# A decoder step on one core: the bias table's chain begun ahead of the first projection step, that step's products reordered, and the squares' gate moved

## The chip, the cores and the metric

The kernel runs on one core of a Trainium2 chip. The metric is the device time of one execution in microseconds; three runs of the kernel before took 2097.12, 2097.62 and 2098.48 us. The engines are called by their names or as the profile shortens them: TensorE (PE, its weight loads PEld), VectorE (DVE), ScalarE (ACT), GpSimd (POOL) and SyncE (SP). DMAs are issued by SP, ACT and POOL and run on 16 DMA engines.

## What is computed

One inference step of a one-layer decoder trunk on 2048 prompt positions with 16 meta tokens ahead of them, and on 8 sample rows. Cut to what matters here:

```python
h = rmsnorm(x, norm1_g)
p = h @ w_in                     # q 512 | k 128 | v 128 | conv a 512 | conv b 512
s = q.k / 8 + rel_bias[t5_bucket(distance)]    # window of 128, 8 heads, learned sinks
o = softmax(s, with sink) @ v
u = a * sigmoid(b)               # then a causal depthwise conv, 31 taps, LayerNorm, swish
x = x + concat(o, c) @ w_out
x = x + relu(rmsnorm(x) @ w_up)**2 @ w_down
y = rmsnorm(x)
```

The relative-position bias is the same table for every block of queries: for each head a row of 384 values by distance, which has to be laid out as a skewed matrix of 128 queries by 256 keys.

## The kernel before

**Tiles and products.** The positions are cut into five tiles (400, 448, 448, 448 and 328 columns); activations lie transposed, channels on partitions, in eight chunks `x[c]`. Weights come in slabs of 128 x 1024 numbers (512 KB): `raw` is loaded by SP, ScalarE casts it to a rounded high part `whi` (line 138), and VectorE subtracts to a low part `wlo` (line 115). Activations are split the same way into `hi` and `lo`. A projection step (`pe_step`) is 24 matmuls into one PSUM buffer: for eight chunks `whi`*`hi`, `whi`*`lo` and `wlo`*`hi`. There are two `raw` buffers, three pairs `whi`/`wlo`, and three PSUM buffers of the kind `mm` (steps 4 and 5 borrow two of another kind). The slabs are called 1, 2, 3 ... here in order of use; step k uses slab k, as long as tile 0 alone is worked on.

**The start.** `norm1_first` loads slab 1, the eight chunks of tile 0 and slab 2, and splits tile 0 times the gain, without its norm. The norm's scale `rs` is worked out beside the first steps: squares on ScalarE (`norm_stats`, held back by a one-element copy from a gate tile), their sum on VectorE (`ss`), column sums on TensorE (`st<-ones,ss`), a root and a reciprocal (`rq`), a diagonal (`m<-idn,rq`), a product that spreads it over the partitions (`st<-m,ones`), and a copy from PSUM by ScalarE (`t<-st`, 128x400). Each step's result of tile 0 waits in PSUM until VectorE has multiplied it by `rs` (`m<-mm,t`); the first such copy frees the PSUM buffer that step 6 needs. Meanwhile GpSimd issues the eight loads of tile 1 (`t<-x_in`), each behind a one-element copy from the last high part of tile 0.

**The bias chain.** `bias_setup` (line 937) multiplies the table by a one-hot matrix on TensorE (`st<-relt`), copies the 8 x 384 result from PSUM with ScalarE, and GpSimd issues its DMAs: `scr` (for the sample rows), `skw` (16 shifted copies in DRAM), one read for the sample rows, and eight reads of `skw` into `bias`, which wait for `skw` to have landed. It is called before the second step (`BAT = 1`). The first user of `bias` is the attention of tile 0 (`attn_gen`, line 576, a VectorE operation that adds it to the scores and takes the maximum).

**The order.** The program is written once, and a scheduler sets each engine's order from it at build time; a part under `high_priority` is drawn ahead. Each engine then works through its own order, and waits at an instruction until its operands are there.

Of the kernel before, what the change touches and what calls it, by code (L numbers as in the profile page):

```python
# [18 lines left out]
NH = 8  # L19
# [60 lines left out]
def trunk(tc, x_in, w_all, smalls, rel, ck, cv, sconv, y_out, kv_out, ck_out, cv_out, up_out, us_out):  # L80
    nc = tc.nc
    with ExitStack() as ctx:
# [10 lines left out]
        def ahead(gen, off, cond=None):  # L93
            while True:
                try:
                    if off and (cond is None or cond()):
                        with tc.high_priority(off):
                            r = next(gen)
                    else:
                        r = next(gen)  # L100
                except StopIteration:
                    return
                yield r
# [39 lines left out]
        def slot(dt=F32, i=None):  # L143
            t = tp.tile([128, TS], dt, tag="t", name="t")
            return t[:, SHIFT[i]:] if i in SHIFT else t
# [45 lines left out]
        def split_slab():  # L191
            k = pos["split"]
            if k >= len(order):
                return
            while pos["dma"] <= k:
                dma_slab()
            r = raws.pop(k)
            hi = sl.tile([128, 8, 128], F32R, tag="whi", name="whi", bufs=NSPL)
            lo = sl.tile([128, 8, 128], F32R, tag="wlo", name="wlo", bufs=NSPL)
            cpy(hi, r)  # L200
            tt(lo, r, f(hi), ALU.subtract)
            split[k] = (hi, lo)
            pos["split"] += 1
# [10 lines left out]
        def pe_step(hi, lo, n, evac, budget, late=False, parts=1, keep=False, spare=False):  # L214
            k = cur[0]
            if not keep:
                cur[0] += 1
            while pos["split"] <= min(k + LA, len(order) - 1):
                split_slab()
            while pos["dma"] < min(k + LA + 1 + NRAW, len(order)):  # L220
                dma_slab()
            if late:
                flush()
            wh, wl = split[k] if keep else split.pop(k)
            if spare:
                ps = pa.tile([128, 512], F32, tag="pt", name="mm")
            else:
                ps = pm.tile([128, 512], F32, tag="mm", name="mm")
            o = ps[:, :n]
            seq = []  # L230
            if late:
                for c in range(8):
                    seq += [(wh, hi, c), (wh, lo, c), (wl, hi, c)]
            else:
                for c in range(8):
                    seq += [(wh, hi, c), (wh, lo, c)]
                seq += [(wl, hi, c) for c in range(8)]
            cut = [len(seq) * (p + 1) // parts for p in range(parts)]
            for j, (w, a, c) in enumerate(seq):
                mm(o, w[:, c, :], a[c], j == 0, j == len(seq) - 1)  # L240
                if j + 1 == cut[0]:
                    old = list(pend)
                    pend.clear()
                    for e in old:
                        e()
                if j + 1 in cut:
                    bg.step(budget / parts)
            pend.append(lambda: evac(ps))
# [68 lines left out]
        def run_stats(gen, box):  # L317
            for r in gen:
                if r is None or r is STEP:
                    yield r  # L320
                else:
                    box.append(r)
# [42 lines left out]
        def norm1_first():  # L365
            s = st[0]
            n = TI[0]
            dma_slab()
            x = s["x"] = load_x(0)
            dma_slab()  # L370
            with tc.high_priority(2000):
                split_slab()
                warm = misc()
                for _ in range(WARM):
                    mm(warm[:, :128], ones, ones, True, True)
                s["h1h"], s["h1l"] = [], []
                for c in range(8):
                    hi = slot(F32R)
                    lo = slot(F32R)
                    act(hi[:, :n], x[c][:, :n], AF.Copy, scale=sm[:, G1 + c:G1 + c + 1])  # L380
                    stt(lo[:, :n], x[c][:, :n], sm[:, G1 + c:G1 + c + 1], f(hi[:, :n]), ALU.mult, ALU.subtract)
                    s["h1h"].append(hi)
                    s["h1l"].append(lo)
            split_slab()
            g1 = norm1_gen(1)
            next(g1)
            box = []
            s["rs"] = slot()
            for _ in ahead(run_stats(norm_stats(x, n, quick="a0" in QUICK, gate=s["h1h"][7], out=s["rs"]), box), 2000):
                pass  # L390
            return g1

# [541 lines left out]
                q.dma_start(y_out[:, YO[i] + c * n:YO[i] + (c + 1) * n], y[:, :n])  # L934
                yield

        def bias_setup():
            ps = misc()
            mm(ps[:NH, :EW], relt[:33, 0:NH], relt[:33, 8:8 + EW], True, True)
            e = slot()  # L940
            cpy(e[:NH, :EW], ps[:NH, :EW])
            nc.gpsimd.dma_start(scr.rearrange("p h x -> h p x"),
                                e[:NH, :EW].unsqueeze(1).broadcast_to([NH, NSMP, EW]))
            a = skw[:]
            row = NH * SKWW
            nc.gpsimd.dma_start(bass.AP(tensor=a.tensor, offset=a.offset, ap=[[SKWW, NH], [row + 1, NSKW], [1, EW]]),
                                e[:NH, :EW].unsqueeze(1).broadcast_to([NH, NSKW, EW]))
            for q in range(0, 128, NSKW):
                nc.gpsimd.dma_start(bias[q:q + NSKW], bass.AP(tensor=a.tensor, offset=a.offset + 127 - q,
                                                              ap=[[row, NSKW], [SKWW, NH], [1, 256]]))  # L950
# [80 lines left out]
        for op in prog:  # L1031
            k = op[0]
            if k == "in":
                _, i, m = op
                if i == 0:
                    if nin == N1AT:
                        gens["n1"] = [bg.add(g1)]
                    if nin == BAT:
                        bias_setup()
                    nin += 1  # L1040
                win_step(i, m, 24 * (TI[i] / 2400.0) - 1.2 - 0.6, spare=i == 0 and nin in (4, 5))
            elif k == "in2":
                m = op[1]
                win_step(0, m, 24 * (TI[0] / 2400.0) - 1.2 - 0.6, keep=True)
                win_step(1, m, 24 * (TI[1] / 2400.0) - 0.6)
            elif k == "conv0":
                flush()
                gens["conv"] = [bg.add(ahead(conv_gen(0), HP0, lambda: "ln" in st[0])), bg.add(conv_pe_gen(0), True)]
            elif k == "attn0":
                flush()  # L1050
                gens["attn"] = [bg.add(attn_gen(0, range(j, PT[0] // BQ[0], NS0)), A0F) for j in reversed(range(NS0))]
            elif k == "out":
                _, i, m = op
                wout_step(i, m, ff_budget(i, False))
            elif k == "ff":
                _, i, t, g, c = op
                b = ff_budget(i, t == "u")
                if t == "u":
                    up_step(i, g * 8 + c, b)
                else:  # L1060
                    down_step(i, g, c, b)
            elif k == "bg":
                i = op[1]
                flush()
                cat_alloc(i)
                gens["attn"] = [bg.add(attn_gen(i, range(j, PT[i] // BQ[i], NS1))) for j in range(NS1)]
                if i == NT - 1:
                    gens["attn"].append(bg.add(sample_gen(i)))
                gens["conv"] = [bg.add(ahead(conv_gen(i), HPC, lambda: "ln" in st[i]))]
            elif k == "sync_bg":  # L1070
                flush()
                bg.drain(gens["attn"] + gens["conv"])
            elif k == "n1":
                gens["n1"] = [bg.add(norm1_gen(op[1]))]
            elif k == "sync_n1":
                bg.drain(gens["n1"])
            elif k == "n2":
                gens["n2"] = [bg.add(ahead(norm2_gen(op[1]), HPN if op[1] else HPN0))]
            elif k == "sync_n2":
                flush()  # L1080
                bg.drain(gens["n2"])
            elif k == "fin":
                gens["fin"] = [bg.add(ahead(final_gen(op[1]), HPF if op[1] == NT - 1 else 0))]
                if op[1] == NT - 1:
                    flush()
                    bg.drain()
# [16 lines left out]
HPN0 = 300  # L1103
HPF = 0
COV = 5
BAT = 1
WARM = 12
N1AT = 3
A0F = True
# [118 lines left out]
```

## Time and profile before

| | |
|---|---|
| runs | 2097.12, 2097.62, 2098.48 us; median 2097.62 |
| profiled execution | 2097.54 us, of which the span is 2095.7 us |
| busy: PE, PEld | 2068.3 us (99%), 1961.5 us (94%) |
| busy: DVE, ACT, POOL | 1525.2 us (73%), 1181.0 us (56%), 55.8 us (3%) |
| chain that ended last | PE 95%, DVE 2%, DMA 1%, ACT 1% |
| granted clock of TensorE, mean | 0.993 |

The span is the time between the first and the last instruction that the profile shows; the execution's own time is 1.8 us longer. Busy times are sums over the whole span; the change touches the first 60 us of it. In the profile's rows a start is in us from the start of the span, and what stands in square brackets is the time for which the engine was idle before the row, and what ended that.

### The profile page before, as it was taken

How to read it: one execution, taken by the hardware profiler on the slowest of the kernel's cores; microseconds unless marked ns; L12 is line 12 of the kernel's file. 1: busy time of each engine (PE TensorE's matmuls, PEld its weight loads, DVE VectorE, ACT ScalarE, POOL GpSimd, SP SyncE). 2: the span in 40 equal slices, each digit the busy share in tenths (PEclk: the TensorE clock that was granted, in tenths of full speed). 3: DMA queues.
4: the chain of work that ended last, by engine and by line, in shares of the span. 5: the costliest groups of instructions: out<-in, count | busy, mean ns of one | idle time of the engine just before them, and what ended most of it. 6: DMA issues, size and time to landing. Idle time of an engine off the chain costs nothing.

```text
span 2095.7 us, 30054 instructions
## 1 busy us (share of the span) xinstructions
PE 2068.3 (99%) x11354; PEld 1961.5 (94%) x11354; DVE 1525.2 (73%) x2603; ACT 1181.0 (56%) x2154; POOL 55.8 (3%) x111
## 2 busy tenths in 40 slices
PE   9899999999999999999999999999999999999998
PEld 8688899999999999999999999999999999999997
DVE  7896798977858987658669886567797754564444
ACT  7577565667456456564454647555646465454443
POOL 3000000000000000000000000000011000000000
PEclk9899999999999999999999999999999999999999
DMA  7113233334532222234323222244433322444443
GB/s 209 47 37 111 100 122 104 128 114 160 179 111 101 101 101 101 101 136 162 129 104 108 101 101 101 101 172 150 142 117 112 123 105 101 151 162 151 151 143 105
DMA packets 77536, 254.39 MB, mean 121 GB/s; under 512 B 9661, under 2 KB 20037, under 8 KB 77392
## 3 DMA queue, kind: packets, MB, share of 16 engines
q1 hardware_dynamic: 72000, 238.08, 32.5%
q0 software_dynamic: 4672, 13.65, 2.3%
q8 instruction: 89, 1.46, 0.3%
q10 hardware_dynamic: 720, 0.76, 0.1%
q14 instruction: 55, 0.45, 0.1%
HBM read 241.97 MB, written 10.47 MB: 120 GB/s over the span
## 4 chain that ended last, share of the span: by engine, by line
PE 95%; DVE 2%; DMA 1%; ACT 1%; issue 0%; POOL 0%; SPq 0%; DVEq 0%; ACTq 0%; POOLq 0%
PE mm L159 89%; PE st L159 2%; PE pt L595 1%; PE s L159 1%; DVE t L119 1%; DMA bias<-skw 0%; DMA skw<-t 0%; DVE t L115 0%; PE cps L159 0%; DVE m L119 0%; ACT p L135 0%; DMA raw<-w_all 0%; DVE p L576 0%; DMA sm<-smalls 0%; ACT L134 0%
## 5 line engine op out<-in xcount | busy, mean ns | idle before, releaser
L159 PE MATMUL mm<-t,whi 128*128 128x448 f32 (+3 forms) x6560 | 1330.9, 349 | 3.1 <-ACT t L138 0.8
L159 PEld LDWEIGHTS mm<-t,whi 128*128 128x128 f32 x6560 | 1164.1, 188 | 58.2 <-DVE t L115 2.9
L138 ACT CAST whi<-raw 128x1024 fp32r<-128x1024 f32 x424 | 443.5, 1049 | 546.6 <-PE mm L159 430.2
L159 PE MATMUL mm<-t,wlo 128*128 128x448 f32 (+3 forms) x3280 | 702.6, 347 | 0.0
L115 DVE TENSOR_TENSOR wlo<-raw,whi 128x1024 fp32r<-128x1024 f32 x424 | 516.6, 1218 | 224.7 <-PE mm L159 123.5
L159 PEld LDWEIGHTS mm<-t,wlo 128*128 128x128 f32 x3280 | 587.9, 188 | 24.9
L119 DVE SCALAR_TENSOR_TENSOR t<-u,sm,t 128x448 f32<-128x448 f32 (+1 forms) x480 | 300.5, 645 | 3.5
L115 DVE TENSOR_TENSOR t<-mm,t 128x448 f32<-128x448 f32 (+2 forms) x200 | 116.5, 583 | 184.5 <-PE mm L159 181.4
L115 DVE TENSOR_TENSOR t<-m,t 128x448 fp32r<-128x448 f32 (+3 forms) x236 | 134.1, 581 | 25.8 <-ACT t L138 25.1
L138 ACT CAST t<-m 128x448 fp32r<-128x448 f32 (+3 forms) x236 | 125.3, 536 | 18.8 <-DVE m L119 14.6
L134 ACT ACTIVATE m<-mm 128x448 f32<-128x448 f32 (+2 forms) x176 | 90.2, 512 | 51.0 <-PE mm L159 49.5
L134 ACT ACTIVATE m<-t 128x448 f32<-128x448 f32 (+3 forms) x140 | 71.7, 542 | 61.7 <-DVE t L115 43.0
L134 ACT ACTIVATE m<-m 128x448 f32<-128x448 f32 (+3 forms) x164 | 90.1, 549 | 4.5 <-DVE m L115 0.6
L135 ACT ACTIVATE p<-p,nm 112x240 f32<-112x240 f32 (+3 forms) x152 | 72.3, 477 | 27.3 <-DVE nm L124 25.9
L576 DVE CUSTOM_DVE_ANT_0 p<-s,bias,sm 112x240 f32<-112x240 f32 (+3 forms) x152 | 61.1, 449 | 6.2 <-DMA bias<-skw 3.8
L134 ACT ACTIVATE p<-p,rd 112x240 f32<-112x240 f32 (+3 forms) x152 | 61.9, 476 | 3.9 <-DVE rd L130 3.5
L115 DVE TENSOR_TENSOR ss<-ss,m 128x448 f32<-128x448 f32 (+3 forms) x100 | 58.4, 584 | 6.3 <-ACT m L134 2.8
L934 POOL DMA_DIRECT2D y_out<-t x32 | 17.3, 543 | 1602.6 <-DVE t L119 1601.4
L130 DVE RECIPROCAL rs<-m 128x448 f32<-128x448 f32 (+2 forms) x15 | 41.6, 2776 | 23.9 <-ACT m L134 23.9
L119 DVE SCALAR_TENSOR_TENSOR t<-t,sm 128x384 f32<-128x384 f32 (+1 forms) x98 | 58.3, 612 | 0.9
L159 PE MATMUL mm<-cal,whi 128*128 128x448 f32 (+2 forms) x160 | 55.3, 347 | 0.2 <-DVE cal L115 0.2
L159 PE MATMUL mm<-cah,whi 128*128 128x448 f32 (+2 forms) x160 | 55.3, 347 | 0.0
(178 smaller groups left out, 1159.6 us busy)
## 6 DMA issues: line engine op xcount, KB each, us to landing
raw<-w_all SPq DMA_DIRECT2D x424, 512.0 KB, 3.2
t<-x_in SPq DMA_DIRECT2D x40, 224.0 KB, 4.6
y_out<-t POOLq DMA_DIRECT2D x24, 224.0 KB, 3.3
t<-x_in SPq DMA_DIRECT2D x16, 164.0 KB, 3.5
t<-x_in POOLq DMA_DIRECT2D x8, 224.0 KB, 4.3
t<-x_in SPq DMA_DIRECT2D x8, 200.0 KB, 4.6
t<-x_in SPq DMA_DIRECT2D x8, 192.0 KB, 3.8
y_out<-t POOLq DMA_DIRECT2D x8, 192.0 KB, 4.7
```

Source lines behind the costliest of these rows:

```text
L115: return nc.vector.tensor_tensor(out, a, b, op=op)
L119: return nc.vector.scalar_tensor_tensor(out, a, s, b, op0=op0, op1=op1)
L130: return nc.vector.reciprocal(out, a)
L134: return nc.scalar.activation(out, a, f, bias=bias, scale=scale)
L135: return nc.scalar.activation(out, a, f, bias=bias, scale=scale, accum_out=accum_out)
L138: return nc.scalar.copy(out, a)
L159: return nc.tensor.matmul(out, lhsT, rhs, start=start, stop=stop)
L576: nc.vector.tensor_tensor_reduce(out=p[:bq, c, :nk], in0=sp[c // 2][:bq, c % 2, :nk], in1=bias[:bq, h, b0:b0 + nk], scale=1.0, scalar=sm[: ...
L595: nc.tensor.transpose(t[:r, c * bq:(c + 1) * bq], p[:bq, c, a:a + r], idn[:bq, :bq])
L934: q.dma_start(y_out[:, YO[i] + c * n:YO[i] + (c + 1) * n], y[:, :n])
```

## The change

Three things. `bias_setup` is called in `norm1_first`, inside the part that is drawn ahead, right behind the split of tile 0, with the last high part as a gate: a one-element copy by GpSimd into the tile that takes the table's copy. Its product goes into a PSUM buffer of the kind that scores use. The first step's 24 products are written in another order: chunk by chunk as the operands come, and no longer all products of `whi` ahead of those of `wlo`. And the squares of tile 0 are gated by the last low part, where it was the last high part. What is computed stays the same.

```diff
@@ pe_step
             seq = []
-            if late:
+            if k == 0:
+                for c in range(9):
+                    if c < 8:
+                        seq += [(wh, hi, c)]
+                    if c > 0:
+                        seq += [(wl, hi, c - 1), (wh, lo, c - 1)]
+            elif late:
                 for c in range(8):
                     seq += [(wh, hi, c), (wh, lo, c), (wl, hi, c)]
@@ norm1_first
                     s["h1h"].append(hi)
                     s["h1l"].append(lo)
+                bias_setup(s["h1h"][7])
             split_slab()
...
-            for _ in ahead(run_stats(norm_stats(x, n, quick="a0" in QUICK, gate=s["h1h"][7], out=s["rs"]), box), 2000):
+            for _ in ahead(run_stats(norm_stats(x, n, quick="a0" in QUICK, gate=s["h1l"][7], out=s["rs"]), box), 2000):
                 pass
@@ bias_setup
-        def bias_setup():
-            ps = misc()
+        def bias_setup(gate):
+            ps = pa.tile([128, 512], F32, tag="s", name="bs")
             mm(ps[:NH, :EW], relt[:33, 0:NH], relt[:33, 8:8 + EW], True, True)
             e = slot()
+            nc.gpsimd.tensor_copy(e[:NH, :1], f(gate[:NH, :1]))
             cpy(e[:NH, :EW], ps[:NH, :EW])
@@ the program's loop
-                    if nin == BAT:
-                        bias_setup()
                     nin += 1
@@ constants
-BAT = 1
```

How this moves instructions is seen in the built programs. GpSimd's queue at the loads of tile 1 (`t<-x_in`, eight in all), before:

```order
L355 DMA t_183<-x_in 128x448
L353 COPY t_195<-t_166 128x1
L355 DMA t_186<-x_in 128x448
L355 DMA t_189<-x_in 128x448
L355 DMA t_192<-x_in 128x448
L355 DMA t_195<-x_in 128x448
L942 DMA scr_97<-t_298 8x8x384
L946 DMA skw_98<-t_298 8x16x384
L634 DMA sbias_14337<-scr_97 64x129
L949 DMA bias_96<-skw_98 16x8x256 x8
```

The same place after:

```order
L361 DMA t_195<-x_in 128x448
L359 COPY t_210<-t_166 128x1
L361 DMA t_198<-x_in 128x448
L361 DMA t_201<-x_in 128x448
L950 DMA scr_97<-t_172 8x8x384
L954 DMA skw_98<-t_172 8x16x384
L361 DMA t_204<-x_in 128x448
L361 DMA t_207<-x_in 128x448
L361 DMA t_210<-x_in 128x448
L641 DMA sbias_14338<-scr_97 64x129
L957 DMA bias_96<-skw_98 16x8x256 x8
```

`scr` and `skw` stood behind all eight loads; they now stand behind the fifth, ahead of the last three.

ScalarE's order from the cast of slab 5 on, before (slabs 5, 6, 7, 8 are raw_314, 354, 399 and 453; `t_198` is `rs`):

```order
L138 CAST whi_395<-raw_314 128x1024
L138 CAST whi_449<-raw_354 128x1024
L134 ACTIVATE rq_236<-st_231,epst_92 128x3
L134 ACTIVATE rq_236<-st_231,epst_92 16x1
L134 ACTIVATE m_242<-idn_85,rq_236 128x128 x3
L134 ACTIVATE m_242<-idn_85,rq_236 16x16
L138 CAST whi_493<-raw_399 128x1024
L138 COPY t_198<-st_241 128x400
L138 CAST whi_545<-raw_453 128x1024
L134 ACT_TABLE_LOAD
L134 ACTIVATE m_325<-m_323 128x400
```

After (slabs 5 to 9 are raw_315, 355, 400, 454 and 498; `t_213` is `rs`):

```order
L138 CAST whi_396<-raw_315 128x1024
L138 CAST whi_450<-raw_355 128x1024
L134 ACTIVATE rq_251<-st_246,epst_92 128x3
L134 ACTIVATE rq_251<-st_246,epst_92 16x1
L134 ACTIVATE m_257<-idn_85,rq_251 128x128 x3
L134 ACTIVATE m_257<-idn_85,rq_251 16x16
L138 CAST whi_494<-raw_400 128x1024
L138 CAST whi_546<-raw_454 128x1024
L138 COPY t_213<-st_256 128x400
L134 ACT_TABLE_LOAD
L134 ACTIVATE m_326<-m_324 128x400
L138 CAST whi_608<-raw_498 128x1024
```

The cast of slab 8 moved from behind the copy of `rs` to ahead of it, and that of slab 9 came up behind the sigmoid's table load.

TensorE at the first step, before, and then after (`t_138`, `t_142`, `t_146` are high parts of chunks 0, 1, 2, `t_139`, `t_143`, `t_147` low parts):

```order
L159 MATMUL mm_271<-t_138,whi_121 128x400
L159 MATMUL mm_271<-t_139,whi_121 128x400
L159 MATMUL mm_271<-t_142,whi_121 128x400
L159 MATMUL mm_271<-t_143,whi_121 128x400
L159 MATMUL mm_271<-t_146,whi_121 128x400
L159 MATMUL mm_271<-t_147,whi_121 128x400
```

```order
L159 MATMUL bs_170<-relt_83 8x384
L159 MATMUL mm_286<-t_138,whi_121 128x400
L159 MATMUL mm_286<-t_142,whi_121 128x400
L159 MATMUL mm_286<-t_138,wlo_122 128x400
L159 MATMUL mm_286<-t_139,whi_121 128x400
L159 MATMUL mm_286<-t_146,whi_121 128x400
L159 MATMUL mm_286<-t_142,wlo_122 128x400
L159 MATMUL mm_286<-t_143,whi_121 128x400
```

The table's product moved ahead of the step, and the `wlo` products in among the others; before, step 1's last nine products stood behind 15 of step 2.

## Rows read from the trace of the kernel before

**Rows 1.** The chain that ended last, first 60 us: start, us, what.

```profile
36.30 7.75 DMA skw<-t
...
48.35 7.81 DMA bias<-skw
```

**Rows 2.** Timeline: start, us, engine, instructions, idle time before and what ended it.

```profile
56.34 0.37 DVE L576 CUSTOM_DVE_ANT_0 p<-s,bias,sm 128x144 f32<-128x144 f32 x1 [3.82 <-DMA bias<-skw]
...
58.19 1.65 PE L159 MATMUL s<-t 128*128 128x144 f32 x6 [6.01 <-DVE t L119]
...
67.31 1.28 DVE L119 SCALAR_TENSOR_TENSOR m<-t,sm,rs 128x448 f32<-128x448 f32 x2 [0.24 <-ACT rs L138]
```

**Rows 3.** Stretches: busy us of PE, PEld, DVE, ACT, POOL; granted clock; DMA.

```profile
54.00:55.00 1.00, 0.00 (x0) 0.00 (x0) 0.00 (x0) 0.00 (x0) 0.00 (x0) 0.74 0.89 197
69.00:75.00 6.00, 6.00 (x19) 5.85 (x20) 5.88 (x13) 2.39 (x6) 0.00 (x0) 0.50 0.00 0
```

**Rows 4.** The same view, the two stretches ahead of the wait.

```profile
30.00:40.00 10.00, 10.00 (x54) 8.95 (x54) 8.85 (x20) 7.95 (x15) 1.24 (x2) 1.00 0.56 121
40.00:50.00 10.00, 10.00 (x58) 10.00 (x58) 9.75 (x16) 9.01 (x20) 4.80 (x9) 1.00 0.75 135
```

**Rows 5.** Timeline of the first 60 us, the steps around `rs`.

```profile
12.21 3.16 PE L159 MATMUL mm<-t,whi 128*128 128x400 f32 x16 [0.66 <-ACT whi L138]
...
14.70 2.13 POOL L355 DMA_DIRECT2D t<-x_in  x4
...
22.10 1.05 ACT L138 CAST whi<-raw 128x1024 fp32r<-128x1024 f32 x1 [3.26 <-DMA raw<-w_all]
...
23.18 1.23 DVE L115 TENSOR_TENSOR wlo<-raw,whi 128x1024 fp32r<-128x1024 f32 x1 [1.99 <-ACT whi L138]
...
24.72 1.05 ACT L138 CAST whi<-raw 128x1024 fp32r<-128x1024 f32 x1 [1.57 <-PE st L159]
...
28.31 1.04 ACT L138 CAST whi<-raw 128x1024 fp32r<-128x1024 f32 x1
...
30.79 0.49 ACT L138 COPY t<-st 128x400 f32<-128x400 f32 x1 [1.44 <-PE st L159]
31.31 2.01 DVE L115 TENSOR_TENSOR m<-mm,t 128x400 f32<-128x400 f32 x4 [0.56 <-ACT t L138]
...
32.12 1.05 ACT L138 CAST whi<-raw 128x1024 fp32r<-128x1024 f32 x1 [0.84 <-PE mm L159]
...
33.41 0.81 PE L159 MATMUL st<-relt 33*8 33x384 f32 x2
...
44.65 4.23 POOL L949 DMA_DIRECT2D bias<-skw  x8 [2.05 <-DMA skw<-t]
```

**Rows 6.** DMA queues, 36.5 to 44.1: packets, MB, share of 16 engines.

```profile
q0 software_dynamic: 206, 0.33, 57.9%
```

**Rows 7.** DMA queues, 45.5 to 53.5.

```profile
q0 software_dynamic: 369, 1.03, 93.7%
```

**Rows 8.** DMA issues, 27.0 to 27.3: count, KB, us to landing.

```profile
raw<-w_all SPq DMA_DIRECT2D x1, 512.0 KB, 3.0
```

**Rows 9.** DMA queues, 49.3 to 53.0 (the only queue with packets).

```profile
q0 software_dynamic: 170, 0.46, 106.1%
```

**Rows 10.** DMA issues, 49.3 to 49.5: count, KB, us to landing.

```profile
raw<-w_all SPq DMA_DIRECT2D x1, 512.0 KB, 7.9
```

**Rows 11.** DMA queues, 17.1 to 19.5.

```profile
q0 software_dynamic: 247, 0.89, 98.7%
q1 hardware_dynamic: 3, 0.00, 0.5%
```

**Rows 12.** DMA queues, 12.0 to 22.1.

```profile
q0 software_dynamic: 517, 1.84, 53.0%
q1 hardware_dynamic: 335, 1.23, 37.0%
```

**Rows 13.** DMA queues, 22 to 37.

```profile
q1 hardware_dynamic: 629, 2.31, 42.8%
```

## The prediction

> **What bounds the kernel now.** TensorE is busy nearly everywhere, so I looked for where it is not. Read in this order: the chain of work that ended last, for the first 60 us; the timeline around its longest pieces; the stretches with the clock; the DMA queues. The chain's first 60 us hold two DMA pieces on the way to the attention bias: the write of `skw` and the last of eight reads into `bias`, 7.8 us each [rows 1]. They end at 56.2, and VectorE, which had nothing else in its order, sat idle 3.82 us for them; TensorE, which needs the queries that VectorE splits behind that wait, sat 6.01 us [rows 2]. In the idle time the granted clock fell to its lower level, 1.2 GHz; 19 products then took 6.0 us, 0.32 us each [rows 3], against 16 in 3.16 us at 2.4 GHz [rows 5].
>
> TensorE is not the bound there, though. VectorE is busy 8.85 and 9.75 us of 10 in the two stretches ahead of the wait [rows 4]. Its run begins when the scale of tile 0 (`rs`) has been copied out of PSUM by ScalarE, 30.79 to 31.28, and the four waiting projection results can be scaled, at 31.31 [rows 5]. From there to the wait its order has 33 operations, nearly without a gap, and after the wait its run goes on as densely. So the start depends on **two times**: when the `rs` copy is done, and when `bias` has landed. The 3.82 us are what the second costs; VectorE's own second wait there, for the next tile's `rs`, is 0.24 us [rows 2], about all that the slow clock cost on VectorE's path. Together 4.1 us is all that an earlier bias can bring.
>
> **The bias chain moved.** It now stands in GpSimd's queue behind five of the eight loads of tile 1. Those loads are issued from 14.70 on at 0.53 us each behind the first four [rows 5], so `scr` goes out at about 15.3 and `skw` at 15.9, 20 us earlier than now. The gate's copy is one element wide, like the eight in the same place. The table's product (0.81 us now, between steps 5 and 6 [rows 5]) goes ahead of step 1, where TensorE waits for operands anyway; ScalarE's copy of the table delays the squares by about half a microsecond, under slabs' casts that wait for their loads. Without that cover they would cost 0.8 and 0.5 us; I cost them at nothing. The three tile-1 loads now behind `scr` and `skw` land some 5 us later and are read only in the second half of VectorE's run. `bias` will have landed by about 37 us, long before its use: the 3.82 us go.
>
> **The first step.** Its 24 products now follow their operands, and fill what was a wait of 0.66 us ahead of step 2 and a piece behind it [rows 5]. It is worth nothing to the end: from 12.2 us up to the norm's column sums TensorE has 64 products before (15 of step 2, nine left over from step 1, 40 more) and 64 after (24 and 24 of steps 2 and 3, 16 of step 4), so the sums begin when they did. The product that spreads `rs` over the partitions comes 29 products later, not 27: at 0.2 us each, 0.4 us later. The squares' later gate (one low part later, some 0.6 us) hides behind the cast of slab 2, which stands ahead of the squares on ScalarE and whose end started step 2 at 12.21 [rows 5].
>
> **What the moved loads collide with.** This is the term that decides. `scr` and `skw` occupied all 16 engines for 57.9% of 7.6 us, 4.4 us in full [rows 6], the eight `bias` reads 93.7% of 8.0 us, 7.5 us [rows 7]. Now they lie between 36 and 56, where weights are prefetched far ahead. After, they lie at 18 to 37, where each slab is cast almost as it lands: slab 5 at 22.10, slab 6 at 24.72, slab 7 at 28.31 [rows 5]; slab 8, issued at 27.1, landed 3.0 us later [rows 8]. And the engines serve what was issued earlier first: a slab issued at 49.3, behind the `bias` reads, moved nothing while those held 106.1% of the next 3.7 us [rows 9] and landed after 7.9 us [rows 10]; slab 5, issued at 17.1, had 3 packets through up to 19.5 while tile 1's loads moved 247 [rows 11].
>
> Step by step (a slab costs about 1.6 us of all engines, from 37.0% of 10.1 us for 1.23 MB; a tile-1 load 0.7 us, 53.0% for eight [rows 12]). Slab 5 goes behind `scr` and `skw`: 22.1 + 4.4 = 26.5. Slab 6 follows at about 28.1. `skw` is behind five loads only; with the 7.8 us that it took and a microsecond behind them it lands at about 24.5, and the `bias` reads are issued from 25.1 to 29, at 0.53 us each [rows 5]. Slab 7 can be issued only when VectorE is done with slab 5 (cast 1.05, low part 1.23 [rows 5]): 28.9. Slab 8 likewise after slab 6: 30.5. Both stand behind all or nearly all `bias` reads, which run from 28.1 to 35.6. Slab 8 lands at 35.6 + 2 x 1.6 = 38.8 us, not at 30.1.
>
> Behind that stands the `rs` copy. **In ScalarE's order the cast of slab 8 used to follow the `rs` copy (32.12 after 30.79 [rows 5]); now it precedes it**, since its buffer is free earlier. So `rs` is done at 38.8 + 1.05 + 0.49 = 40.3, not 31.28: 9.0 us later. All 33 VectorE operations wait for it, and TensorE too: step 6 needs a PSUM buffer that only the first scaled copy frees, so it stands from about 33 to 41. Before, the clock fell 2.3 us into such an idle time (52.2 to 54.5, [rows 3]); it will fall here. Step 6's 24 products then take 7.7 us at 0.32, and VectorE's low part of slab 9, which reuses that step's buffer and now stands 5.3 us into its run (the first scaled copy 0.5, a low part 1.2, four more copies at 0.5, three conv operations at about 0.5), waits for step 6's end, 0.6 + 7.7 = 8.3 us into it: 3.0 us more, or less if the clock is back before that end; I take 2.5.
>
> Sum: -3.8 - 0.2 + 9.0 + 2.5 = **+7.5 us** on the profiled execution's 2097.54 (span 2095.70, the rest lies around it; the median of the runs is 2097.62): 2105.0. One of the sums of squares moves behind the wait; the work is the same. What follows has no tie to absolute time, so the shift reaches the end.
>
> Bounds. The new waits appear in no row. From below: if `scr` and `skw` held slab 5 back by only half, slab 8 lands at about 36 and `rs` is 6 us late: +4.5 with the clock's 2.5. From above: the slowest engine (`skw` landed 7.8 us after its issue [rows 1], for 4.4 us of all engines) adds 1 us and the clock another: +9.5. I take the middle, since both slabs that were issued behind other transfers [rows 9, 11] waited for nearly all of them.
>
> **Rivals.** *The engines take turns.* If each engine alternated between the two queues packet by packet, a slab of 8 packets an engine would meet 8 `bias` packets of about 0.47 us (7.5 us over 16 an engine): 8 x (0.2 + 0.47) = 5.4 us, and with the latency land some 6.2 us after its issue. Slab 5 is then late by about 2, slab 8 is issued at 28.5, lands at 34.7, `rs` is 5 us late, the clock still falls: -4.0 + 5 + 2 = +3, **2100.5** (2098 to 2102). Against it: 3 packets against 247, and none against 170 [rows 9, 11]; for it speak those 3 alone. The Trainium skill, "DMA: Bandwidth & Descriptors", section "Queues, rings and completion order", has this rule: an engine goes round-robin between queues with work, a packet at a time. By that rule it would be this rival; the trace agrees with it nowhere that a slab was issued behind full queues [rows 9, 11].
>
> *The bias loads are out of the way* (the other side: not slower). If the chain drains before slab 8 needs the engines, `rs` moves by the 0.4 us of two products alone and all of the wait is saved: -3.8 - 0.2 + 0.4 = -3.6, **2093.9** (2092.5 to 2096). It speaks for it that slabs keep the 16 engines only 42.8% busy from 22 to 37 [rows 13]. It decides at 4 us: with `rs` less than 4 us late (slab 8 landed by 34, the clock kept), the change is not slower. Against it: slab 8 cannot be issued before 27.1, as now, and by then about four `bias` reads are out.
>
> *The clock stays low.* Before it was low from 54.5 to 75, also while TensorE was full [rows 3]. If it lasts as long here, steps 6 to 8 run at 0.32 and TensorE, not VectorE, ends the stretch: +9.5 to +12, **2108**.
>
> **How the numbers follow.** Forecast (first issued, first served) 0.55, 2102 to 2107; taking turns 0.20; out of the way 0.15; clock stays low 0.07; the rest 0.03 on either side. The predicted time is 2105.0. The range 2094.0 to 2107.5 takes in the forecast, the turns and half of the gain; 0.15 is left out. About 0.2%, 4.2 us, is what a measurement can tell. Slower by more: 0.50 of the forecast, 0.02 of the turns, 0.07 of the clock: 0.59. Faster by more: a third of the gain and some of the rest, 0.08. Within: 0.33.
>
> **What would show it.** In the changed kernel: VectorE's wait for `bias` at the first score gone; slab 5's cast near 26.5, slab 8's near 39; the `rs` copy right behind it near 40; TensorE idle some 8 us from 33 and the clock at 1.2 GHz from 35; the first score near 64. If slab 8 lands by 32 and `rs` by 33, the queue argument is wrong and the kernel is some 2 us faster; if slabs 7 and 8 land about 6 us after issue, engines take turns.

## The result, and the profile after

The changed kernel took 2111.6 us (median of four: 2109.27, 2109.62, 2113.57, 2113.63), the kernel before beside it 2097.7: a ratio of 1.0066, 95% interval 1.0048 to 1.0083. It is slower by 14 us, not by the 7.5 forecast, and outside the range of 2094.0 to 2107.5. The profiled execution is the one of 2113.63 us, with a span of 2111.6.

The chain of work that ended last, first 60 us of the changed kernel (start, us, what):

```profile
21.40 12.00 DMA raw<-w_all
...
35.83 7.30 DMA raw<-w_all
...
43.23 1.04 ACT whi L138
44.27 0.40 ACT t L138
...
45.33 6.92 PE mm L159 x24
```

Before, `skw` and `bias` stood here [rows 1]; now it is slabs: slab 6, issued at 21.4 and landed at 33.4, slab 8, the `rs` copy, and step 6. The timeline of the same stretch (start, us, engine, instructions, idle time before and what ended it; rows between are left out):

```profile
16.19 0.64 POOL L950 DMA_DIRECT2D scr<-t  x1
16.82 0.62 POOL L954 DMA_DIRECT2D skw<-t  x1
25.95 2.67 POOL L957 DMA_DIRECT2D bias<-skw  x5 [2.70 <-DMA skw<-t]
26.96 1.04 ACT L138 CAST whi<-raw 128x1024 fp32r<-128x1024 f32 x1 [6.85 <-DMA raw<-w_all]
33.50 1.04 ACT L138 CAST whi<-raw 128x1024 fp32r<-128x1024 f32 x1 [5.50 <-DMA raw<-w_all]
36.37 2.04 PE L159 MATMUL st<-m,ones 128*128 128x128 f32 x8 [4.26 <-ACT m L134]
41.16 1.04 ACT L138 CAST whi<-raw 128x1024 fp32r<-128x1024 f32 x1 [4.06 <-DMA raw<-w_all]
43.23 1.04 ACT L138 CAST whi<-raw 128x1024 fp32r<-128x1024 f32 x1 [1.03 <-DMA raw<-w_all]
44.18 0.48 ACT L138 COPY t<-st 128x400 f32<-128x400 f32 x1
45.33 5.46 PE L159 MATMUL mm<-t,whi 128*128 128x400 f32 x16 [5.62 <-DVE m L115]
52.32 1.23 DVE L115 TENSOR_TENSOR wlo<-raw,whi 128x1024 fp32r<-128x1024 f32 x1 [2.34 <-PE mm L159]
67.16 0.36 DVE L583 CUSTOM_DVE_ANT_0 p<-s,bias,sm 128x144 f32<-128x144 f32 x1
```

The four casts are those of slabs 5 to 8, at 22.10, 24.72, 28.31 and 32.12 before [rows 5]. The `rs` copy ends at 44.67 where it ended at 31.28. The first score, 56.34 before [rows 2], starts at 67.16 and waits for nothing: the wait for `bias` is gone, and the first score is 10.8 us later all the same.

The granted clock fell again, as it had before [rows 3]: between 36 and 37 us (0.86 on average there), behind 4.26 us in which TensorE was idle and ahead of 5.62 more. The view of stretches; the last three numbers of a row are the granted clock, the DMA share and GB/s:

```profile
33.00:36.00 3.00, 0.00 (x0) 0.00 (x0) 1.35 (x3) 1.43 (x4) 0.56 (x2) 1.00 1.05 157
37.00:45.00 8.00, 2.71 (x9) 1.91 (x8) 1.68 (x6) 2.90 (x5) 0.00 (x0) 0.50 0.51 107
45.00:50.00 5.00, 4.67 (x14) 4.62 (x15) 4.91 (x9) 1.50 (x2) 0.00 (x0) 0.50 0.54 193
51.00:70.00 19.00, 15.07 (x87) 14.93 (x86) 17.30 (x31) 15.66 (x32) 0.00 (x0) 1.00 0.24 84
```

To see where time is lost, I matched VectorE's operations of both traces by name and count. Those of the changed kernel are 10.8 us late at the first score and 10.5 at 100 us, but 15.3 at 300 us and from there on. So **there are two losses**: the one at the start, and 4.8 us near 170 us, outside the first 60 us, which were all that the change was thought to touch. There ScalarE scales the last softmax blocks of tile 0 (`p<-p,rd`, eight) and makes the last copy of its convolution (`t<-cps,sm`), from which the convolution's norm starts. The timeline there, before:

```profile
158.44 0.58 ACT L134 ACTIVATE t<-cps,sm 128x384 f32<-128x384 f32 x1
159.35 3.31 ACT L134 ACTIVATE p<-p,rd 128x256 f32<-128x256 f32 x8 [0.33 <-DVE rd L130]
160.54 3.66 PE L159 MATMUL mm<-t,whi 128*128 128x448 f32 x16
```

and after:

```profile
169.44 3.31 ACT L134 ACTIVATE p<-p,rd 128x256 f32<-128x256 f32 x8 [0.89 <-DVE rd L130]
172.78 0.58 ACT L134 ACTIVATE t<-cps,sm 128x384 f32<-128x384 f32 x1
173.39 0.56 DVE L115 TENSOR_TENSOR m<-m,t 128x384 f32<-128x384 f32 x1 [3.53 <-ACT t L134]
173.89 0.79 PE L159 MATMUL st<-ph,vv 128*128 128x512 f32 x1 [2.24 <-ACT ph L138]
175.18 5.95 PE L159 MATMUL mm<-t,whi 128*128 128x448 f32 x16
```

The two have changed places on ScalarE. VectorE stands 3.53 us for the copy, TensorE stands 2.24 us, and the clock falls once more (0.52 from 173 to 180): the 16 products take 5.95 us, not 3.66.

### The profile page after: what moved, and what is told of

Read it like the earlier page. It is cut to its first block, busy times and chain, and to the rows that moved or that the text cites. A ratio compares the mean times of both kernels' runs of the same rounds, so it can differ in the third digit from the quotient of the medians.

```text
span 2111.6 us, 30058 instructions
## 1 busy us (share of the span) xinstructions
PE 2073.9 (98%) x11354; PEld 1967.8 (93%) x11354; DVE 1524.8 (72%) x2603; ACT 1180.8 (56%) x2154; POOL 56.2 (3%) x112
## 4 chain that ended last, share of the span: by engine, by line
PE 94%; DVE 3%; DMA 2%; ACT 1%; issue 0%; SPq 0%; DVEq 0%; ACTq 0%
PE mm L159 88%; PE st L159 2%; DMA raw<-w_all 1%; PE s L159 1%; PE pt L602 1%; DVE t L119 1%; DVE t L115 0%; DVE m L119 0%; DVE wlo L115 0%; PE cps L159 0%; ACT p L135 0%; ACT whi L138 0%; DVE p L583 0%; DVE ss L115 0%; DMA sm<-smalls 0%
```

## The experiments

What each run's profile shows, in one table. Landings, the end of the `rs` copy and the first score are us from the start of the span; in brackets the first score less VectorE's wait for `bias`. The shift is how much later VectorE's operations start than in the kernel before, at 100 and at 300 us. A trace shows one execution, and the last two columns say which one: its time, and the median of all runs.

| kernel | slabs 6, 7, 8 land | `rs` | first score | shift | traced run | median |
|---|---|---|---|---|---|---|
| before | 24.6, 27.6, 30.1 | 31.3 | 56.3 (52.5) | | 2097.5 | 2097.6 |
| changed | 33.4, 41.1, 43.1 | 44.7 | 67.2 | +10.5, +15.3 | 2113.6 | 2111.6 |
| changed, again | 32.8, 40.2, 42.5 | 44.0 | 66.7 | +10.1, +13.5 | 2111.4 | 2113.6 |
| chain only | 33.7, 40.4, 42.5 | 42.0 | 62.5 | +6.7, +6.6 | 2105.0 | 2101.2 |
| step and gate only | 25.2, 29.7, 32.3 | 33.9 | 56.3 (54.3) | 0.0, 0.0 | 2098.3 | 2099.2 |
| reads after `rs` | 29.7, 32.0, 36.1 | 37.6 | 59.2 | +2.5, +4.3 | 2102.1 | 2104.3 |
| conv copy first | 34.0, 38.4, 39.6 | 41.2 | 62.9 | +6.3, +6.4 | 2104.3 | 2108.4 |
| `rs` copy first | 36.8, 41.1, 42.5 | 41.7 | 62.7 | +7.2, +6.8 | 2104.3 | 2104.3 |
| chain after `rs` | 25.2, 29.6, 32.1 | 31.6 | 54.4 (53.6) | -2.6, -2.6 | 2095.8 | 2095.3 |
| the same again | 24.7, 28.0, 30.3 | 31.2 | 53.3 | -3.7, -3.7 | 2094.6 | 2095.0 |
| chain after diagonal | 24.8, 29.0, 31.3 | 31.5 | 55.5 | -1.5, -1.5 | 2096.9 | 2096.3 |
| chain after root | 25.0, 29.6, 32.4 | 31.2 | 53.7 | -3.2, -3.2 | 2095.1 | 2095.9 |
| the same again | 25.0, 29.3, 31.6 | 31.4 | 53.4 | -3.6, -3.6 | 2094.4 | 2095.3 |

In all but one of these profiles the first score, less its wait, comes 20.4 to 22.7 us after the `rs` copy (24.0 with the chain after the diagonal, for a reason below). So the time of that copy decides most of the first loss.

**The chain alone.** The step's order and the gate go back to what they were; only the chain is moved.

```diff
-            if k == 0:
...
-            elif late:
+            if late:
...
-            for _ in ahead(run_stats(norm_stats(x, n, quick="a0" in QUICK, gate=s["h1l"][7], out=s["rs"]), box), 2000):
+            for _ in ahead(run_stats(norm_stats(x, n, quick="a0" in QUICK, gate=s["h1h"][7], out=s["rs"]), box), 2000):
```

> The changed kernel with the first step's products and the squares' gate as before; only the bias chain is moved. On ScalarE the copy of `rs` now stands ahead of slab 8's cast, and the last conv copy of tile 0 (`t<-cps`) ahead of the softmax scaling (`p<-p,rd`), both as before the change; `scr` and `skw` stand behind six of tile 1's loads. Theory (the DMAs collide, and a second loss comes from ScalarE's order near 170 us): slabs 6 and 7 still land near 33 and 41, so `rs` is copied near 41.7 and not 44.2, the first score is 8 us late, and no further loss comes near 170: 2105, between 2103 and 2107. Rival A (the order on ScalarE is the cause, not the DMAs): slab 7 lands by 31, `rs` near 32, the wait for `bias` is gone: 2094. Rival B (the 15 us all come from the DMAs, none from 170): 2111.

Ratio 1.0021 (1.0011 to 1.0030), median 2101.2. The timeline, slabs 6 and 7 and `rs`:

```profile
33.75 1.04 ACT L138 CAST whi<-raw 128x1024 fp32r<-128x1024 f32 x1 [6.27 <-DMA raw<-w_all]
40.53 1.05 ACT L138 CAST whi<-raw 128x1024 fp32r<-128x1024 f32 x1 [3.17 <-DMA raw<-w_all]
41.48 0.49 ACT L138 COPY t<-st 128x400 f32<-128x400 f32 x1
```

The trace is the theory's: slabs as late as in the changed kernel, the `rs` copy at 41.5 ahead of slab 8's cast, no second loss. The time is not: this profiled execution took 2105.0, the longest of ten, and the median is 3.8 us below it and below the forecast range. The ten lie 2.6 to 7.4 us above the median of the kernel before; what was shorter in the other nine isn't shown, since only this one has a trace. Rival A (the order, not the DMAs) falls by the slabs, rival B by the missing second loss.

**Step and gate alone**, the chain where it was; against the kernel before:

```diff
-            if late:
+            if k == 0:
...
+            elif late:
...
-            for _ in ahead(run_stats(norm_stats(x, n, quick="a0" in QUICK, gate=s["h1h"][7], out=s["rs"]), box), 2000):
+            for _ in ahead(run_stats(norm_stats(x, n, quick="a0" in QUICK, gate=s["h1l"][7], out=s["rs"]), box), 2000):
```

> The kernel before with the first step's products and the squares' gate as in the changed kernel; the bias chain stays where it was. Slab 8's cast precedes the copy of `rs` on ScalarE, as in the changed kernel. Theory: without the chain's DMAs slab 8 lands near 30, `rs` is copied near 31.7, at most 1 us late, and the wait for `bias` of 3.8 us takes that up: 2097.6, between 2097 and 2099. Rival A (the order on ScalarE costs, whatever the DMAs do): `rs` several us late, 2102 or more.

Ratio 1.0008 (0.9999 to 1.0018): 1.6 us slower at the median, not told apart from nothing. `rs` was 2.6 us late, more than expected, since slab 8, whose cast now stands ahead of it, landed at 32.3; the wait for `bias` took it up (2.06 us instead of 3.82), and the first score stands where it stood. So the order on ScalarE is hidden here rather than free: less that wait, the first score would come at 54.3 and not at 52.5. With the chain moved, the wait is gone and the slabs are late, and it shows: the chain alone costs 3.6 us at the median, all three parts 14 to 16. At 170 us the order is the old one in this run, as with the chain alone; only all parts together turned it round.

**The reads out of the crowded stretch.**

```diff
+            bias_read(s["rs"])
             return g1
...
+        def bias_read(gate):
...
+            nc.gpsimd.tensor_copy(bias[:, 0, :1], f(gate[:, :1]))
             for q in range(0, 128, NSKW):
```

> The changed kernel, every engine's order the same, but the eight reads into `bias` wait behind a one-element copy from `rs` on GpSimd. So only `scr`, `skw` and tile 1's loads are left to collide with slabs 5 to 8. Theory (each transfer in the crowded stretch adds its share, reads 7.5 us of 16 engines, `scr` and `skw` 4.4): slab 5 still lands near 26.9, slabs 6 to 8 land about 5 us sooner than in the changed kernel, `rs` near 38; the reads then run from 39 to 47, ahead of the first score: first score 5 to 6 us late instead of 10.8, and the late loss near 170 stays, since ScalarE's order is the same: 2106, between 2103 and 2108. Rival C (the reads did no harm, `skw` and tile 1's loads decide): `rs` stays near 43, 2110 or more.

Ratio 1.0034 (1.0021 to 1.0047), median 2104.3, in the theory's range; rival C falls. The traced execution is the shortest of six, and its first score is 2.9 us late, not 5 to 6. Timeline, slabs 5 to 8 and `rs`:

```profile
26.49 1.05 ACT L138 CAST whi<-raw 128x1024 fp32r<-128x1024 f32 x1 [7.96 <-DMA raw<-w_all]
29.82 1.05 ACT L138 CAST whi<-raw 128x1024 fp32r<-128x1024 f32 x1 [2.29 <-DMA raw<-w_all]
33.34 1.03 ACT L138 CAST whi<-raw 128x1024 fp32r<-128x1024 f32 x1
36.18 1.04 ACT L138 CAST whi<-raw 128x1024 fp32r<-128x1024 f32 x1 [1.81 <-DMA raw<-w_all]
37.13 0.49 ACT L138 COPY t<-st 128x400 f32<-128x400 f32 x1
```

Slab 5 is as late as in the changed kernel, so that is not the reads' doing; `scr`, `skw` and tile 1's loads are what is left. The second loss is there, at 1.8 us (2.5 to 4.3). Slabs 6 and 7 land 3.7 and 9 us sooner than in the changed kernel. Its second run (below) is the nearer match: slab 5 landed at 26.4 in both, and slab 6 was issued at 20.2 here and at 19.8 there. DMA issues of slabs 6 and 7 (the last number is us to landing), with the reads held back:

```profile
raw<-w_all SPq DMA_DIRECT2D x1, 512.0 KB, 9.5
...
raw<-w_all SPq DMA_DIRECT2D x1, 512.0 KB, 3.2
```

and with the reads, in the changed kernel's second run:

```profile
raw<-w_all SPq DMA_DIRECT2D x1, 512.0 KB, 13.0
...
raw<-w_all SPq DMA_DIRECT2D x1, 512.0 KB, 11.5
```

The first read was issued at 25.6 there, so the reads **held back a slab that was issued 5.8 us ahead of them**. How the two queues shared the engines in the changed kernel's first run is seen in the DMA queues, first from 25.9 to 33.4 (packets, MB, share of 16 engines):

```profile
q0 software_dynamic: 306, 0.87, 59.3%
q1 hardware_dynamic: 189, 0.69, 42.0%
```

then from 33.4 to 41.1:

```profile
q1 hardware_dynamic: 196, 0.70, 50.0%
q0 software_dynamic: 183, 0.48, 41.2%
```

Both queues move packets all the time, in the second stretch nearly one for one.

**The conv copy first.** The second loss, taken alone: every order up to 170 us stays, and there the softmax scaling waits for the copy.

```diff
+                    if i == 0 and b == blocks[-1] and kv == 1:
+                        while 3 not in s["cvs"]:
+                            yield STEP
+                        nc.vector.tensor_copy(rd[:1, :1], s["cvs"][3][:1, :1])
                     tt(dn[:bq], dn[:bq], es[:bq], ALU.add)
                     recip(rd[:bq], dn[:bq])
```

> The changed kernel with one dependence more: a one-element copy on VectorE lets the softmax scaling of tile 0's last blocks (`p<-p,rd`, eight on ScalarE, near 170 us) wait for the copy of the last conv channel (`t<-cps`). Every engine's order up to there is that of the changed kernel; from there ScalarE makes the conv copy first, as before the change. Theory (a second loss comes from that order): the first score is as late as in the changed kernel, VectorE's shift against the kernel before is the same at 100 us and at 300 us, and the time is 3 to 4.5 us below the changed kernel's: 2107.5, between 2106 and 2109. Rival B (the shift near 170 comes from the clock or a DMA, not from that order): the same as the changed kernel, 2110 to 2113.

**The changed kernel again**, beside it.

> The changed kernel once more, beside the others. Theory: again two levels some 4 us apart, as its first four runs (2109.3, 2109.6 and 2113.6, 2113.6), median 2109 to 2113; in a run of the lower level VectorE's shift between 100 us and 300 us is under 1 us.

With the copy first: 2108.4, ratio 1.0048 (1.0033 to 1.0063). Again: 2113.6, ratio 1.0076 (1.0061 to 1.0091), above the range expected. The two intervals overlap only from 1.0061 to 1.0063; the traces decide. The one with the copy first is of the shortest of four executions, 4.1 us below their median: its start (6.3 us late) is not that of a usual one. Timeline with the copy first:

```profile
165.63 0.58 ACT L134 ACTIVATE t<-cps,sm 128x384 f32<-128x384 f32 x1 [1.25 <-PE cps L159]
167.16 3.31 ACT L134 ACTIVATE p<-p,rd 128x256 f32<-128x256 f32 x8 [0.95 <-DVE rd L130]
167.31 3.67 PE L159 MATMUL mm<-t,whi 128*128 128x448 f32 x16
```

The shift is 6.3 at 100 us and 6.4 at 300: no second loss. In the repeated run it is 10.1 and 13.5, so rival B falls. That run's profile is the shortest of its four (2111.36), and the second loss is in it too, against what I expected of a lower level. Its size differs by the clock: the same 16 products there,

```profile
174.79 4.47 PE L159 MATMUL mm<-t,whi 128*128 128x448 f32 x16
```

4.47 us, where the first profile had 5.95 and the kernel with the copy first 3.67. That is 1.5 of the 2.3 us between the two profiled executions of the changed kernel. With the reads held back ScalarE's order is the changed one too, VectorE stands 3.53 us for the copy as well, but the clock stayed at 1.00 there:

```profile
166.60 3.67 PE L159 MATMUL mm<-t,whi 128*128 128x448 f32 x16
```

and the second loss is 1.8 us. So the order alone costs 1.8 us; of the 3.0 and 1.6 us more in the two profiles of the changed kernel, 2.3 and 0.8 are in these 16 products at a lower clock. That the pairs among the changed kernel's times are made by this clock alone isn't shown.

**The `rs` copy ahead of the slabs' casts**, on top of the conv copy.

```diff
+            if k in (6, 7):
+                cpy(hi[:1, 0, :1], st[0]["rs"][:1, :1])
             cpy(hi, r)
```

> As the kernel with the conv copy first, and the casts of slabs 7 and 8 on ScalarE wait for the copy of `rs` (a one-element copy from it into their tile); the DMAs are issued in the order of the changed kernel. So `rs` is copied as soon as its spread is there. Theory (both the order on ScalarE and the late slabs hold VectorE): `rs` is done near 37.5 instead of 41 to 44, VectorE scales its first four results at once and then waits for slab 7's and slab 8's low parts, whose slabs land near 39 to 43 as before: 2 to 3 us less than with the conv copy first: 2105.5, between 2104 and 2107. Rival E (only the place of the `rs` copy behind slab 8's cast costs, the slabs could be late without harm): all of the 4 to 6 us come back, 2102 or less. Rival F (only the slabs count): 2108 as with the conv copy first.

Ratio 1.0035 (1.0022 to 1.0049), median 2104.3: 4 us less than with the conv copy alone, in the theory's range. The profile shows another course, though:

```profile
36.85 1.05 ACT L138 CAST whi<-raw 128x1024 fp32r<-128x1024 f32 x1 [3.94 <-DMA raw<-w_all]
41.17 0.49 ACT L138 COPY t<-st 128x400 f32<-128x400 f32 x1 [0.70 <-PE st L159]
41.92 2.00 ACT L138 CAST whi<-raw 128x1024 fp32r<-128x1024 f32 x2
```

In this execution slab 6 took 15.5 us and landed at 36.8. The root for `rs` follows slab 6's cast on ScalarE, so `rs` was late by slab 6 itself. Rivals E and F fall by the times (2103.8 to 2105.3), but that the casts' place was worth 4 us is not shown by a trace. Nor is it shown why the median stays 3 us above that of the chain alone, which has the same two orders.

**The chain sooner, but behind `rs`, behind the diagonal, or behind the root**, with step and gate as before the change. Against the chain alone, behind `rs`:

```diff
-                bias_setup(s["h1h"][7])
...
+            bias_setup(s["rs"])
             return g1
```

and instead of that last call, in `rstd`, behind the diagonal (behind the root the same two lines stand a step sooner, with `r`):

```diff
                 mm(ps[:, o], ones[:w], dg[:w, o], True, True)
+            if out is not None:
+                bias_setup(dg)
             yield STEP
```

> The kernel before with the whole chain behind `rs`: ScalarE copies the table right behind the copy of `rs`, and `scr`, `skw` and the reads follow, some 3 to 4 us sooner than before the change; first step and squares' gate as before. Theory: slabs 5 to 8 land as before the change, `rs` is copied near 31.3, `skw` is issued near 32.5 instead of 36.3, `bias` lands near 52, and the wait of 3.82 us shrinks to under 0.5: 2094, between 2093 and 2096. Rival D (a bias chain that comes sooner costs wherever it stands, by the slabs that it delays): 2097 or more.

> As the chain behind `rs`, but gated one step sooner, by the diagonal (`m<-idn,rq`) that spreads `rs`: ScalarE copies the table near 29.5, ahead of the copy of `rs`, `skw` is issued near 30.5 instead of 33.4. Theory: slabs 5 to 7 are landed or nearly so by then, `rs` is copied at 31.1 to 31.6, `bias` lands near 51, and no wait for it is left: 1 us less than with the chain behind `rs`: 2094, between 2093 and 2095. Rival D (sooner costs wherever it stands): 2096 or more.

> One step sooner still, gated by the root (`rq`): the table is copied ahead of slab 7's cast, near 27, and `skw` is issued near 28. Theory (what is on the engines delays the slabs around it, whichever was issued first, but only slabs up to 7 stand ahead of the copy of `rs` here): slab 7, issued at 26.4, lands 1 to 3 us late, `rs` with it, and the wait for `bias` is gone: 2095.5, between 2094 and 2097.5. First issued, first served: slab 7 is untouched, `rs` near 31.5, 2094 as with the diagonal.

> The chain behind `rs` once more, in more rounds, beside the kernel before: 2095.3, 2 us below it, between 2094.5 and 2096.

> The chain behind the root once more, in more rounds: within 1 us of the chain behind `rs` on either side, 2095.5, between 2094.5 and 2096.5.

Ratios: behind `rs` 0.9988 (0.9979 to 0.9998), again 0.9991 (0.9983 to 1.0000); diagonal 0.9994 (0.9984 to 1.0003); root 0.9994 (0.9984 to 1.0003), again 0.9993 (0.9984 to 1.0001). Behind `rs` the kernel is about 2 us faster than before the change, though the second interval reaches 1.0000; it is faster than the changed kernel too. Behind the diagonal and the root the medians are 1.0 to 1.8 us below the kernel before, and the intervals don't tell them apart from it. Rival D falls behind `rs` and behind the root; behind the diagonal the median, 2096.3, is in rival D's range and not in the theory's. Behind the root slab 7 was to be late and was not (issued at 26.2, landed at 29.6): `scr` was issued only at 29.5, so that theory wasn't put to the test. In the repeated run behind `rs` the first score (timeline) waits for nothing:

```profile
30.69 0.49 ACT L138 COPY t<-st 128x400 f32<-128x400 f32 x1 [1.27 <-PE st L159]
32.84 0.63 POOL L948 DMA_DIRECT2D skw<-t  x1
53.27 0.37 DVE L577 CUSTOM_DVE_ANT_0 p<-s,bias,sm 128x144 f32<-128x144 f32 x1
```

In its first run 0.85 us of the wait was left. Behind the diagonal the wait is gone too, but the first score is 2 us later than here. Its timeline has the reason:

```profile
51.53 1.04 ACT L138 CAST whi<-raw 128x1024 fp32r<-128x1024 f32 x1 [3.35 <-DMA raw<-w_all]
52.60 1.23 DVE L115 TENSOR_TENSOR wlo<-raw,whi 128x1024 fp32r<-128x1024 f32 x1 [1.85 <-ACT whi L138]
```

Slab 11, issued at 43.1 among the reads, landed at 51.5 (49.2 in the run above) and held VectorE for 1.85 us. That is what rival D says, one place further on.

## Why the prediction was wrong, point by point

**Right.** What bounds the kernel there: the first score follows the `rs` copy and `bias`, in every profile of the table. The wait for `bias` went (-3.8), though `bias` landed at 42.1 and not by 37. The chain's new place collides with slabs 5 to 8, and the loss is on the path through `rs`: slab 5 cast at 26.96 for 26.5, slab 8's cast ahead of the `rs` copy. That slab 5 came out so well is in part luck: it landed at 26.4 to 26.9 in four of the six traces with the early chain, and at 30.5 and 31.8 in the other two. The clock fell between 36 and 37 for 35 and was back at 1.00 from 51, so the rival in which it stays low falls; VectorE's low part of slab 9 waited 2.34 us for step 6, for 2.5.

**The term that was mis-sized: "+9.0 us (`rs` late)".** It measured +13.4. The step that failed is "the engines serve what was issued earlier first". By it slab 6 was to land at 28.1, ahead of all reads. It landed at 33.4, so that VectorE was done with it, and slab 8 could be issued, at 35.8 and not at 30.5. Slab 8 then took 7.3 us, a little less than forecast, and landed at 43.1 for 38.8; slab 7, issued at 29.3 for 28.9, landed at 41.1, still ahead of it. So the 4.4 us by which the term fell short are slab 6's 5.3 less about 1 of slab 8. In the five traces with the chain's reads in that stretch slab 6 landed at 32.8 to 36.8, with the reads held back at 29.7; the 1.6 us from 28.1 to 29.7 aren't theirs. The two rows on which the rule stood [rows 9, 11] are both of a slab issued behind reads or loads that were already there; neither shows a slab issued ahead. That was an argument from one side.

The rival of turns came nearer here, though not in its numbers: it put slabs 7 and 8 about 6 us after their issue, and they took 11.8 and 7.3, slab 7 with slab 6 still ahead of it in its own queue up to 33.4. The Trainium skill ("DMA: Bandwidth & Descriptors", section "Queues, rings and completion order") has an engine take turns between queues a packet at a time, and gives some 9 to 17 descriptors as a packet's usual size. The rival read that as one packet of the trace a turn, and so read, 196 and 183 packets from 33.4 to 41.1 agree, 189 and 306 less, 3 against 247 [rows 11] and none against 170 [rows 9] not at all. But the trace counts each 4 KB row of a slab as a packet. Over 16 engines 247 are 15 an engine and 170 are 11, within one packet as the Trainium skill counts, so these rows don't speak against its rule, as the prediction said they did. What sets the shares is open; no run here separates turns from the dearer packets shown at the end.

**The term for the clock: "+2.5".** Net +1.3: 22.5 us from the `rs` copy to the first score, for 21.2. The wait was there, but one operation of 0.6 us fewer stood in the run (32 for 33), and two gaps of 0.25 us had gone.

So the start adds up: -3.82 + 13.39 + 1.25 = +10.82, as measured at the first score. The "-0.2" didn't come: VectorE waits 0.24 us for the next tile's `rs` in the changed kernel too.

**The step that was left out: "What follows has no tie to absolute time, so the shift reaches the end."** It cost 4.8 us in the first profile and 3.4 in the second, by another order on ScalarE at 170 us; with that order mended it is 0.1. The order of the changed kernel could be read before the prediction; I compared it only around the start. The last 0.8 us of the 16.1 between the profiled executions isn't followed up.

**The first step "is worth nothing to the end", and the gate "hides".** Alone they hide, behind the wait for `bias`, which the change takes away. Together with the chain they cost: the chain alone keeps both of ScalarE's old orders and costs 3.6 us, all three parts 14. Of that difference the traces show the second loss (3.4 to 4.8 us) and an `rs` copy 2.0 to 2.7 us later behind slab 8's cast; the rest isn't shown.

## What to carry to other kernels

A transfer moved to where others are consumed as they land has to be priced against every transfer in flight, also those issued ahead of it, and by what packets cost beside it, not by what they cost elsewhere. Where a scheduler sets the orders, compare them to the end and not only around the edit: the parts of the change together turned two instructions round 150 us later, which neither the chain alone nor the other two parts alone did, and that cost a quarter to a third of the loss. And a gain was there to be had, by moving the chain some 3 us and not 20.

## What the runs showed of the hardware that I had not expected

A slab's packet costs more while the reads run. From 33.4 to 41.1 the slabs' 196 packets took 50.0% of 16 engines for 7.7 us, 0.31 us each. With the reads held back, from 29.9 to 32.0, where slabs had the engines to themselves:

```profile
q1 hardware_dynamic: 135, 0.49, 69.3%
```

0.17 us each, much as before the change (335 packets in 37.0% of 10.1 us, 0.18 us each [rows 12]). It is not other traffic as such. From 25 to 29 us of the same run, while tile 1's loads moved 114 packets in the other queue:

```profile
q1 hardware_dynamic: 179, 0.64, 40.0%
```

0.14 us each. So my 1.6 us for a slab does not hold beside these reads: there it was 1.8 times as much. Why is open. The last load of tile 1, which stands ahead of the reads in GpSimd's own queue, took 12.9 us in both profiles of the changed kernel and 11.0 with the reads held back.

The size of the loss also changed between executions with nearly the same DMA order up to there: slab 5, issued at 17.5 to 17.9 in all six traces with the early chain, took 8.5 to 9.3 us in four of them and 12.7 and 14.2 in two. The times alone would not show it: they spread over 4.8 us for the chain alone and 5.4 for the changed kernel, but over 4.4 in 22 runs of the kernel before too.
